# A two-block model on one core: wide feed-forward products, later assumed landings, more idle products at two norms

## Chip, core and metric

One core of a Trainium2 chip runs the whole program, in fp32 data with TensorE's products on operands of type fp32r. The metric is the device time of one execution in microseconds (us). The kernel before was run three times: 1648.75, 1653.19 and 1653.45 us, median 1653.19.

## What is computed

A sequence of 256 tokens of width 1024 goes through a first block (a mixer made of a recurrence and dilated attention, then a feed-forward network) and two second blocks (feed-forward, mixer, feed-forward each). So there are eight sublayers, 0 to 7: mixers are 0, 3 and 6, feed-forward networks 1, 2, 4, 5 and 7. A feed-forward network with its norms and its modulation is, cut to what matters:

```python
h = modulate(rms_norm(x, g_pre), shift, scale)
u, gt = split(h @ w_in, 2)          # 1024 -> 2 x 2816
f = (silu(u) * gt) @ w_out          # 2816 -> 1024
x = x + gate * rms_norm(f, g_post)  # the second block has no rms_norm on f
```

shift, scale and gate come from a product of a condition vector with a matrix (`w_ada`), 24 chunks of 128 values per sublayer.

## The kernel before, in words

Activations lie transposed: a tile is 128 features by 256 tokens. To keep fp32 accuracy every operand is split in two: `hi`, the value rounded by ScalarE to fp32r, and `lo`, what is left, by a subtraction on VectorE (`split`, `load_split`). A product of weights w and activations x is then three matmuls into the same sum, `mm3` (L1022): hi(w)·hi(x), hi(w)·lo(x), lo(w)·hi(x), each with 128x128 weights and 256 moving columns. In the profile's names the weights are `hi` and `lo`; the activations of a network's input are `hh` and `hl` (or `UH` and `UL`, see below), those of its output product `fh` and `fl` (the last eight `fg`), those of a mixer's output `oh` and `ol`.

Weights come in transfers of 512 KB (`raw`, four row chunks by 256 columns), issued in order on SP's queue from one list for the whole program; `fetch` keeps three split ones ahead. Between them stand the transfers of the modulation rows (`ada_step`, from `in_ada`, also 512 KB), each of which VectorE multiplies with the condition and sums (`junk`). None are left for the last feed-forward network.

A feed-forward network (`ffn`, L1253) has NF = 22 units. A unit is a pair of column chunks, one of u and one of gt, over 8 row chunks. The first three units run on `UH`/`UL`, which is x times its scale before the norm's factor is known (`pair_u`, 258 columns); the norm's factor is multiplied in afterwards. The other 19 use `pair` (L1027): the two sums lie side by side in one PSUM bank with the tag `mm`, of which there are two. Behind each unit ScalarE takes silu of the one half (`su`), VectorE multiplies with the other (`fy`), and the result is split (`fh`, `fl`). Then `out_proj` (L1208) makes four pairs of output chunks over 22 row chunks; the last pair uses a bank of `mm` and one of `a`, so that the two end apart.

In the first block (sublayers 0 and 1) the output goes through a norm: a sum over the squares by TensorE into a bank `c`, a logarithm and an exponential on ScalarE (`rstd`), then VectorE multiplies and adds chunk by chunk (`f`, `x`), and ScalarE makes the next `UH`. Meanwhile TensorE runs idle products whose result nobody reads (`keep_warm`, L1123), 14 of 128x256.

The order of the instructions isn't that of the code. All calls on the engines are recorded (`_Engine.record`, L722), with a cost and a time until the result can be used; per sublayer `emit` (L898) tries orders on a model of the engines (`_Stretch.run`) and takes the one with the best score. Each engine then executes its list in order. All recorded instructions therefore have one line in the profile, L725, and are told apart by their tiles.

Of the kernel before, what the change touches and what calls it, by code (L numbers as in the profile page):

```python
# [12 lines left out]
F32 = mybir.dt.float32  # L13
# [12 lines left out]
D = 1024  # L26
# [7 lines left out]
EXPM05 = float(np.exp(np.float64(-0.5)))  # L34

# [582 lines left out]
class _Model:  # L618


    def __init__(self):
        self.at = {"pe": 0.0, "dve": 0.0, "act": 0.0, "pool": 0.0, "dma": 0.0}
        self.uses, self.slots = {}, {}
        self.rec = None
# [54 lines left out]
class _Engine:  # L679
# [42 lines left out]
    def record(self, op, f, a, k):  # L722
# [3 lines left out]
        if op == "dma_start":  # L726
# [3 lines left out]
            if self.name == "dma":  # L730
                return rec.add(_Op("dma", emit, n / 360e3, 0.0), [out], src)
# [56 lines left out]
class _Kernel:  # L788
# [93 lines left out]

    def split(self, y, hi, lo):

        self.act(hi, y)
        self.tt(lo, y, hi.bitcast(F32), SUB)
# [11 lines left out]
    def emit(self, tag, cx):  # L898
# [24 lines left out]
        for stay, lead in rec.starts(tag):  # L923
# [5 lines left out]
            if __import__("os").environ.get("DBG"): print(tag, stay, lead, round(new[0],1), round(best[3],1))  # L929
# [92 lines left out]
    def mm3(self, out, wh, wl, xh, xl, first, last):  # L1022
        self.mm(out, wh, xh, first, False)
        self.mm(out, wh, xl, False, False)
        self.mm(out, wl, xh, False, last)

# [140 lines left out]
    def scaled(self, sub, pool, tag):  # L1167

        self.G = [self.t(pool, [128, S], tag % j) for j in range(KC)]
# [7 lines left out]
    def chunk_hl(self, n, m, j, pool=False):  # L1177
        h = self.t(self.hp, [128, S], "hh%d" % j, F32R)
        l = self.t(self.hp, [128, S], "hl%d" % j, F32R)
        ins = self.act(h, n, AF.Identity, bias=m[:, j:j + 1])  # L1180
        if pool:
            self.nc.gpsimd.tensor_scalar(n, n, 1.0, m[:, j:j + 1], MUL, ADD)
            self.ptt(l, n, h.bitcast(F32), SUB)
        else:
            self.stt(l, n, m[:, j:j + 1], h.bitcast(F32), ADD, SUB)
# [22 lines left out]
    def out_proj(self, nk, H, L, sub, fpool=None):  # L1208
# [21 lines left out]
        for p in range(4):  # L1230
            ps = self.pair(nk, H, L, last=p == 3)
            for c in range(2):
                j = 2 * p + c
                pc = ps[c] if p == 3 else ps[:, c * S:c * S + S]
# [7 lines left out]
        if fpool is not None:  # L1242
            r = self.rstd(self.sums)
            self.behind_r = self.r_ins
            self.keep_warm(14, H[0], self.sums)
# [7 lines left out]
    def ffn(self, sub, n):  # L1253
        tc, nc = self.tc, self.nc
        n_u = 3
        with ExitStack() as rx:
# [4 lines left out]
            def gated(k, y):  # L1261
                h = self.t(fp, [128, S], "fh%d" % k, F32R)
                l = self.t(fp, [128, S], "fl%d" % k if k < NF - KC else "fg%d" % (k - NF + KC), F32R)
                self.split(y, h, l)
# [30 lines left out]
            for k in range(n_u, NF):  # L1295
                if sub == 2 and k == 8:
                    self.rope2_tables(self.pool(rx, "rt2"))
                ps = self.pair(KC, self.H, self.L)
                su = self.t(ft, [128, S], "su")
                self.act(su, ps[:, :S], AF.Silu)  # L1300
                y = self.t(ft, [128, S], "fy")
                self.tt(y, ps[:, S:], su, MUL)
                gated(k, y)
            self.use_table(LNEXP)
            self.out_proj(NF, hh, hl, sub, fp if sub < 2 else None)
            self.emit(sub + 3, rx)

# [84 lines left out]
    def token_loads(self, w, H, L, views, post):  # L1392
# [5 lines left out]
        def quantum(k, q):  # L1398
            def f(hi, lo):
# [3 lines left out]
                for x, (xh, xl) in enumerate(zip(views(H[k]), views(L[k]))):  # L1403
# [13 lines left out]
    def start(self, late):  # L1417
# [15 lines left out]
        for k in range(KC):  # L1433
# [6 lines left out]
            h = self.t(self.hp, [128, S], "hh%d" % k, F32R)  # L1440
# [1027 lines left out]
```

## Time and profile before

| | |
|---|---|
| three runs | 1648.75, 1653.19, 1653.45 us |
| the profiled execution | 1650.98 us |
| its span, first to last instruction | 1648.9 us |
| mean granted clock of TensorE | 0.992 of full |
| TensorE busy | 1581.3 us, 14250 matmuls |
| VectorE busy | 1234.8 us |
| ScalarE busy | 962.2 us |
| moved by DMA | 359.64 MB, mean 218 GB/s |

The profile is of one execution. Busy time of an engine is the union of its instructions; matmuls are pipelined, so that each is shown longer (some 0.28 us) than the distance of their starts. A group of instructions by line shows its count, busy time, mean length and the idle time of the engine ahead of it, with what ended that.

### The profile page before, as it was taken

Reading aid. Unit: us, or ns where it says so; the run is one execution under the profiler, and the core shown is the slowest. Engines: PE = TensorE matmul, PEld = TensorE weight load, DVE = VectorE, ACT = ScalarE, POOL = GpSimd, SP = SyncE. Lnnn points to the kernel's source line nnn. Section 1 sums busy time; section 2 is a strip of 40 time slices with the busy share of each in tenths; the row PEclk is TensorE's granted clock in tenths of the full one; section 3 lists DMA queues with packets and bytes.
Section 4 is the critical chain, followed back from the end, with each engine's and each line's share of the span. In section 5 each row is a group of like instructions: output and inputs, shape, how many; then the busy total and the mean of one; then the engine's idle time right before and its main releaser. Section 6 shows DMA issues by size and latency. Waiting matters only on the chain. (4 is left out here: it accounts for less than half of the span.)

```text
span 1648.9 us, 35735 instructions
## 1 busy us (share of the span) xinstructions
PE 1581.3 (96%) x14250; PEld 1495.3 (91%) x14250; DVE 1234.8 (75%) x2547; ACT 962.2 (58%) x1851; POOL 18.5 (1%) x39
## 2 busy tenths in 40 slices
PE   4999999989999899999999999999999999999998
PEld 4988888889999899999788999999999978899997
DVE  6897775687777797787869877778768887875544
ACT  5674554767444474445697744456454569874542
POOL 0010000000000000000000000000000000000001
PEclk9999999989999999999999999999999999999999
DMA  9645354465888858888524588876888753255552
GB/s 363 254 141 195 101 182 147 134 220 181 292 290 290 285 199 299 281 298 280 173 92 145 184 294 296 277 278 214 300 274 302 278 170 116 82 168 198 182 174 95
DMA packets 102696, 359.64 MB, mean 218 GB/s; under 512 B 11392, under 2 KB 13056, under 8 KB 102528
## 3 DMA queue, kind: packets, MB, share of 16 engines
q1 hardware_dynamic: 102528, 357.34, 63.6%
q8 instruction: 112, 1.84, 0.5%
q14 instruction: 56, 0.46, 0.1%
HBM read 356.25 MB, written 1.05 MB: 217 GB/s over the span
## 5 line engine op out<-in xcount | busy, mean ns | idle before, releaser
L725 DVE TENSOR_TENSOR lo<-raw,hi 128x1024 fp32r<-128x1024 f32 (+2 forms) x478 | 556.3, 1184 | 187.4 <-issue 75.9
L725 ACT ACTIVATE hi<-raw 128x1024 fp32r<-128x1024 f32 (+2 forms) x478 | 486.8, 1026 | 350.7 <-PE ps_mm L725 254.4
L725 PE MATMUL ps_mm<-hh,hi 128*128 128x256 f32 x2040 | 510.0, 286 | 19.2 <-ACT hh L725 9.2
L725 PE MATMUL ps_mm<-hl,hi 128*128 128x256 f32 x2040 | 505.2, 285 | 0.0
L725 PEld LDWEIGHTS ps_mm<-hh,hi 128*128 128x128 f32 x2040 | 387.4, 192 | 27.7 <-DVE fy L725 12.0
L725 PEld LDWEIGHTS ps_mm<-hl,hi 128*128 128x128 f32 x2040 | 387.2, 192 | 2.0 <-issue 0.8
L725 PE MATMUL ps_mm<-hh,lo 128*128 128x256 f32 x2040 | 316.7, 286 | 0.0
L725 DVE CUSTOM_DVE_ANT_0 junk<-raw,cond 128x1024 bf16<-128x1024 f32 x192 | 235.6, 1227 | 64.0 <-DMA raw<-in_ada 63.3
L725 PEld LDWEIGHTS ps_mm<-hh,lo 128*128 128x128 f32 x2040 | 275.7, 193 | 2.9 <-issue 1.1
L725 PE MATMUL ps_mm<-fh,hi 128*128 128x256 f32 x770 | 188.9, 281 | 0.0
L725 PEld LDWEIGHTS ps_mm<-fh,hi 128*128 128x128 f32 x770 | 144.5, 188 | 0.9 <-DVE fy L725 0.9
L725 PE MATMUL ps_mm<-fl,hi 128*128 128x256 f32 x490 | 120.4, 280 | 0.0
L725 PE MATMUL ps_mm<-fh,lo 128*128 128x256 f32 x770 | 115.5, 281 | 2.5 <-DVE lo L725 2.5
L725 PEld LDWEIGHTS ps_mm<-fh,lo 128*128 128x128 f32 x770 | 102.0, 188 | 2.8 <-DVE lo L725 2.8
L725 ACT ACTIVATE fh<-fy 128x256 fp32r<-128x256 f32 x110 | 44.9, 412 | 94.1 <-DVE fy L725 94.1
L725 PEld LDWEIGHTS ps_mm<-fl,hi 128*128 128x128 f32 x490 | 92.2, 188 | 0.0
L725 PE MATMUL ps_mm<-fg,hi 128*128 128x256 f32 x280 | 69.4, 281 | 0.0
L725 PE MATMUL ps_a<-UH,hi 128*128 128x258 f32 x168 | 49.4, 297 | 6.1 <-ACT UH L725 6.1
L725 PEld LDWEIGHTS ps_mm<-fg,hi 128*128 128x128 f32 x280 | 52.7, 188 | 0.0
L725 ACT ACTIVATE su<-ps_mm 128x256 f32<-128x256 f32 x95 | 35.6, 375 | 29.0 <-PE ps_mm L725 28.9
L725 ACT ACTIVATE UH<-x,mod 128x256 fp32r<-128x256 f32 x56 | 26.4, 501 | 43.6 <-DVE x L725 43.6
L725 PE MATMUL ps_a<-UL,hi 128*128 128x258 f32 x168 | 48.9, 293 | 0.0
(559 smaller groups left out, 2631.3 us busy)
## 6 DMA issues: line engine op xcount, KB each, us to landing
raw<-in_ffi SPq DMA_DIRECT2D x220, 512.0 KB, 5.4
raw<-in_ada SPq DMA_DIRECT2D x192, 512.0 KB, 5.3
raw<-in_ffo SPq DMA_DIRECT2D x100, 512.0 KB, 5.1
raw<-in_win SPq DMA_DIRECT2D x66, 512.0 KB, 4.3
raw<-in_wout SPq DMA_DIRECT2D x24, 512.0 KB, 4.1
w<-in_cw SPq DMA_DIRECT2D x16, 512.0 KB, 8.0
raw<-in_ws SPq DMA_DIRECT2D x16, 448.0 KB, 7.5
raw<-in_ffo SPq DMA_DIRECT2D x20, 256.0 KB, 4.0
```

The source lines that it names most:

```text
L725: emit = lambda: f(*a, **k)
```

## The change

It has three parts. In the feed-forward networks' input products behind the first three units, and in the first three output pairs, hi(w)·hi(x) and hi(w)·lo(x) become one matmul of 512 columns: the two halves of an activation now lie in one tile of 128 x 2 x 256 (`parts`), the product writes a whole bank, first half and second half, and lo(w)·hi(x) adds to the first half (`pair_wide`). Each of a pair's two sums then has a bank of its own, both of one tag, and `mm`, `a` and `b` take turns. `halves` adds the two halves of a bank: ScalarE copies the second to SBUF (`wa`), VectorE adds the first. Second, while a feed-forward network is recorded, the ordering model takes a weight transfer to be usable 0.7 us later than its cost says, and one of modulation rows 2 us later. Third, `keep_warm` is called with 34 instead of 14, for both output norms of the first block. The mixers' activations use the new tiles too, but are multiplied as before. The core of the diff:

```diff
 SHIFT = 2560
 HP = HS = 0
 EXPM05 = float(np.exp(np.float64(-0.5)))
+
+
+def low(x):
+
+    return x[:, 1] if len(x.shape) == 3 else x
 
 
 
...
             src = [aps[1]] if aps[1].space == SBUF else []
             n = out.nbytes() if callable(out.nbytes) else out.nbytes
             if self.name == "dma":
-                return rec.add(_Op("dma", emit, n / 360e3, 0.0), [out], src)
+                lag = 0.0
+                if self.model.late_dma and out.shape[-1] == D:
+                    lag = 2.0 if rec.group == 12 else 0.7
+                return rec.add(_Op("dma", emit, n / 360e3, lag), [out], src)
             return rec.add(_Op(self.name, emit, 0.06, 2.2 + n / 360e3), [out], src)
         if not aps:
             return rec.add(_Op(self.name, emit, 1.28, 0.0), [], [])
...
         o, w = self.vat[name]
         return self.vect[:, o + j:o + (w if n is None else j + n)]
 
+    def halves(self, ps, pool):
+
+        t = self.t(pool, [128, S], "wa")
+        self.act(t, ps[:, S:], AF.Copy)
+        self.tt(t, ps[:, :S], t, ADD)
+        return t
+
     def split(self, y, hi, lo):
 
         self.act(hi, y)
...
 
     def mm3(self, out, wh, wl, xh, xl, first, last):
         self.mm(out, wh, xh, first, False)
-        self.mm(out, wh, xl, False, False)
+        self.mm(out, wh, low(xl), False, False)
         self.mm(out, wl, xh, False, last)
+
+    def pair_wide(self, nk, H, L):
+
+
+        tag = self.wide[0]
+        self.wide.rotate(-1)
+        ps = [self.psum(tag) for c in range(2)]
+        for r in range(0, nk, 4):
+            m = min(4, nk - r)
+            hi, lo = self.fetch()
+            for q in range(m):
+                k = r + q
+                for c in range(2):
+                    w = slice(q * 256 + c * 128, q * 256 + c * 128 + 128)
+                    self.mm(ps[c], hi[:, w], L[k].rearrange("p a b -> p (a b)"), k == 0, False)
+                    self.mm(ps[c][:, :S], lo[:, w], H[k], False, k == nk - 1)
+        return ps
+
+    def parts(self, pool, tag, t=None):
+
+        t = self.t(pool, [128, 2, S], tag, F32R) if t is None else t
+        return t[:, 0], t
 
     def pair(self, nk, H, L, tag="mm", last=False):
 
...
 
     def scaled(self, sub, pool, tag):
 
-        self.G = [self.t(pool, [128, S], tag % j) for j in range(KC)]
+        def two(j):
+            g = self.t(pool, [128, 2, S], tag % j)
+            return g[:, 0], g[:, 1]
+
+        self.G = [g for j in range(KC // 2) for g in two(j)]
         for j, g in enumerate(self.G):
             self.act(g, self.x[j], AF.Copy, scale=self.mod(sub)[:, 8 + j:9 + j])
 
...
             rec.late = 0.0
 
         for p in range(4):
-            ps = self.pair(nk, H, L, last=p == 3)
+            two = wide is not None and p < 3
+            ps = self.pair_wide(nk, H, L) if two else self.pair(nk, H, L, last=p == 3)
             for c in range(2):
                 j = 2 * p + c
-                pc = ps[c] if p == 3 else ps[:, c * S:c * S + S]
+                pc = ps[c] if two or p == 3 else ps[:, c * S:c * S + S]
+                if two:
+                    pc = self.halves(pc, wide)
                 if fpool is None:
                     update(j, pc)
                 else:
...
         if fpool is not None:
             r = self.rstd(self.sums)
             self.behind_r = self.r_ins
-            self.keep_warm(14, H[0], self.sums)
+            self.keep_warm(34, H[0], self.sums)
             self.new_sum()
             for j in range(KC):
                 self.tt(f[j], f[j], r, MUL)
...
     def ffn(self, sub, n):
         tc, nc = self.tc, self.nc
         n_u = 3
+        self.model.late_dma = True
+        self.wide = deque(("mm", "a", "b"))
         with ExitStack() as rx:
             fp, ft = (self.pool(rx, "ffn%d%d" % (n, b), b) for b in (1, 2))
             hh, hl = [], []
             pend = []
 
             def gated(k, y):
-                h = self.t(fp, [128, S], "fh%d" % k, F32R)
-                l = self.t(fp, [128, S], "fl%d" % k if k < NF - KC else "fg%d" % (k - NF + KC), F32R)
-                self.split(y, h, l)
+                h, l = self.parts(fp, "fh%d" % k if k < NF - 4 else "fg%d" % (k - NF + 4))
+                self.split(y, h, low(l))
                 hh.append(h)
                 hl.append(l)
 
...
             for k in range(n_u, NF):
                 if sub == 2 and k == 8:
                     self.rope2_tables(self.pool(rx, "rt2"))
-                ps = self.pair(KC, self.H, self.L)
+                ps = [self.halves(p, ft) for p in self.pair_wide(KC, self.H, self.L)]
                 su = self.t(ft, [128, S], "su")
-                self.act(su, ps[:, :S], AF.Silu)
+                self.act(su, ps[0], AF.Silu)
                 y = self.t(ft, [128, S], "fy")
-                self.tt(y, ps[:, S:], su, MUL)
+                self.tt(y, ps[1], su, MUL)
                 gated(k, y)
             self.use_table(LNEXP)
-            self.out_proj(NF, hh, hl, sub, fp if sub < 2 else None)
+            self.out_proj(NF, hh, hl, sub, fp if sub < 2 else None, ft)
             self.emit(sub + 3, rx)
+        self.model.late_dma = False
 
 
     def weave(self, streams, dense=None, share=0.0):
```

What this does to the order is shown at three places. TensorE, in the feed-forward network of sublayer 2, a stretch of the input products; before (`hh` and `hl` are the halves of a chunk, the number tells the chunk's tile):

```order
L725 MATMUL ps_mm<-hh_7750,hi 128x256
L725 MATMUL ps_mm<-hl_7751,hi 128x256
L725 MATMUL ps_mm<-hh_7750,hi 128x256
L725 MATMUL ps_mm<-hl_7751,hi 128x256
L725 MATMUL ps_mm<-hh_7755,hi 128x256
L725 MATMUL ps_mm<-hl_7756,hi 128x256
L725 MATMUL ps_mm<-hh_7755,hi 128x256
L725 MATMUL ps_mm<-hl_7756,hi 128x256
```

and with the change, in the same network:

```order
L732 MATMUL ps_b<-hh_7427,hi 128x512 x2
L732 MATMUL ps_b<-hh_7428,hi 128x512 x2
L732 MATMUL ps_b<-hh_7422,lo 128x256 x2
L732 MATMUL ps_b<-hh_7423,lo 128x256 x2
L732 MATMUL ps_b<-hh_7427,lo 128x256 x2
L732 MATMUL ps_b<-hh_7428,lo 128x256 x2
```

Two matmuls of 256 columns per chunk and sum have become one of 512, now into banks of `b`; the `lo` products stay 256 wide and follow in runs. In all there are 5 x 436 products fewer and 40 idle ones more.

VectorE, in the network of sublayer 4, before:

```order
L725 TENSOR_TENSOR fy<-ps_mm,su 128x256
L725 TENSOR_TENSOR lo<-raw,hi 128x1024
L725 TENSOR_TENSOR fl_12289<-fy,fh_12288 128x256
L725 TENSOR_TENSOR lo<-raw,hi 128x1024
L725 TENSOR_TENSOR fy<-ps_mm,su 128x256
L725 TENSOR_TENSOR lo<-raw,hi 128x1024 x2
L725 TENSOR_TENSOR fl_12302<-fy,fh_12301 128x256
```

and with the change:

```order
L732 TENSOR_TENSOR fy<-wa,su 128x256
L732 TENSOR_TENSOR fh_11676<-fy,fh_11676 128x256
L732 ISA junk,mod_9951<-raw,cond 128x1024
L732 ISA mod_9951 128x1
L732 TENSOR_TENSOR lo<-raw,hi 128x1024 x4
L732 TENSOR_TENSOR wa<-ps_b,wa 128x256 x2
L732 ISA junk,mod_9951<-raw,cond 128x1024
L732 ISA mod_9951 128x1
```

The two additions `wa` of a unit are new; they stand together behind a run of weight splits, and `fy` reads their result and not PSUM.

SP's queue, at the joint of the networks of sublayers 1 and 2 (`in_ffo` are output weights, `in_ffi` input weights, `in_ada` modulation rows), before:

```order
L725 DMA raw<-in_ffo 128x512
L725 DMA raw<-in_ada 128x1024 x2
L725 DMA raw<-in_ffi 128x1024
L725 DMA raw<-in_ada 128x1024
L725 DMA raw<-in_ffi 128x1024
L725 DMA raw<-in_ada 128x1024
L725 DMA raw<-in_ffi 128x1024 x5
```

and with the change:

```order
L732 DMA raw<-in_ffo 128x512
L732 DMA raw<-in_ada 128x1024
L732 DMA raw<-in_ffi 128x1024
L732 DMA raw<-in_ada 128x1024
L732 DMA raw<-in_ffi 128x1024
L732 DMA raw<-in_ada 128x1024 x5
L732 DMA raw<-in_ffi 128x1024 x5
```

Behind the last output weights seven transfers of modulation rows stand ahead of the third input weights, where there were four.

## Rows read from the trace of the kernel before

**Rows 1.** The page: busy time of the engines, and TensorE's clock in 40 slices.

```profile
PE 1581.3 (96%) x14250; PEld 1495.3 (91%) x14250; DVE 1234.8 (75%) x2547; ACT 962.2 (58%) x1851; POOL 18.5 (1%) x39
...
PEclk9999999989999999999999999999999999999999
```

**Rows 2.** Busy time by stretch, input products: stretch, length, engines, clock, DMA share, GB/s.

```profile
597.90:702.70 104.80, 104.14 (x866) 103.29 (x865) 82.00 (x130) 52.73 (x80) 0.00 (x0) 1.00 0.81 279
938.90:1044.10 105.20, 104.30 (x867) 103.25 (x865) 79.82 (x121) 53.21 (x78) 0.00 (x0) 1.00 0.83 283
...
1472.10:1577.00 104.90, 104.21 (x866) 103.25 (x865) 58.76 (x83) 53.26 (x77) 0.00 (x0) 1.00 0.57 188
```

**Rows 3.** The same view, two stretches of output products.

```profile
702.60:765.50 62.90, 62.90 (x530) 62.85 (x530) 49.47 (x73) 28.05 (x38) 0.00 (x0) 1.00 0.81 275
...
1577.00:1639.80 62.80, 62.80 (x529) 62.80 (x530) 30.21 (x37) 24.28 (x31) 4.84 (x7) 1.00 0.43 142
```

**Rows 4.** Timeline of TensorE, 1040 to 1060: start, us, what, count.

```profile
1040.08 3.98 PE L725 MATMUL ps_mm<-hh,lo 128*128 128x256 f32 x32
...
1055.52 3.00 PE L725 MATMUL ps_mm<-fh,lo 128*128 128x256 f32 x24
```

**Rows 5.** Timeline of TensorE, 957 to 960; fourteen steps between second and third.

```profile
957.38 0.38 PE L725 MATMUL ps_mm<-hh,hi 128*128 128x256 f32 x1
957.61 0.28 PE L725 MATMUL ps_mm<-hl,hi 128*128 128x256 f32 x1
...
959.21 0.28 PE L725 MATMUL ps_mm<-hl,hi 128*128 128x256 f32 x1
959.32 1.07 PE L725 MATMUL ps_mm<-hh,lo 128*128 128x256 f32 x8
```

**Rows 6.** Timeline of TensorE, the mixers' 512-column products; twelve steps between second and third.

```profile
820.42 0.86 PE L725 MATMUL ps_mm<-lo,hh 128*128 128x512 f32 x3
1349.04 0.39 PE L725 MATMUL ps_mm<-hi,hh 128*128 128x512 f32 x1
...
1351.80 0.39 PE L725 MATMUL ps_mm<-hi,hh 128*128 128x512 f32 x1
...
1353.37 1.53 PE L725 MATMUL ps_mm<-lo,hh 128*128 128x512 f32 x6
```

**Rows 7.** Timeline of all engines at the second output norm.

```profile
565.96 2.02 PE L725 MATMUL ps_c<-fh 128*128 128x256 f32 x14
...
567.30 2.77 DVE L725 TENSOR_TENSOR f<-f,rstd 128x256 f32<-128x256 f32 x8 [2.09 <-ACT rstd L725]
569.99 2.77 DVE L725 TENSOR_TENSOR x<-f,x 128x256 f32<-128x256 f32 x8
570.45 3.31 ACT L725 ACTIVATE UH<-x,mod 128x256 fp32r<-128x256 f32 x8 [3.18 <-DVE x L725]
571.01 0.58 PE L725 MATMUL ps_a<-UH,hi 128*128 128x258 f32 x1 [3.03 <-ACT UH L725]
```

**Rows 8.** Groups by line, ScalarE, 938.9 to 1044.1: count, busy, mean ns, idle before.

```profile
L725 ACT ACTIVATE hi<-raw 128x1024 fp32r<-128x1024 f32 x38 | 40.3, 1060 | 29.3 <-PE ps_mm L725 26.6 <-DMA raw<-in_ffi 2.7
...
L725 ACT ACTIVATE su<-ps_mm 128x256 f32<-128x256 f32 x18 | 6.8, 375 | 5.6 <-PE ps_mm L725 5.6
```

**Rows 9.** Waits of VectorE from 938.9 to 1044.1.

```profile
DVE junk L725 <- DMA raw<-in_ada: 6.7, 5, 2.0
```

**Rows 10.** Waits of TensorE in the whole span: us, times, longest.

```profile
PE ps_mm L725 <- DVE fy L725: 7.6, 11, 1.9
...
PE ps_mm L725 <- DVE lo L725: 2.5, 1, 2.5
```

**Rows 11.** Busy time by stretch of 4 us at the two output norms.

```profile
364.00:368.00 4.00, 4.00 (x20) 4.00 (x20) 4.00 (x11) 3.85 (x11) 0.00 (x0) 0.50 0.22 87
368.00:372.00 4.00, 4.00 (x26) 3.92 (x25) 2.38 (x7) 2.92 (x5) 0.00 (x0) 0.80 0.02 4
...
572.00:576.00 4.00, 4.00 (x26) 4.00 (x25) 4.00 (x12) 3.29 (x10) 0.00 (x0) 0.70 0.84 339
```

More of the change, by code (lines that the diff above doesn't have):

```diff
@@ L621, in __init__ @@
     def __init__(self):
+        self.late_dma = False
         self.at = {"pe": 0.0, "dve": 0.0, "act": 0.0, "pool": 0.0, "dma": 0.0}
@@ L928, in emit @@
             best = improve(new, best, stay)
-            if __import__("os").environ.get("DBG"): print(tag, stay, lead, round(new[0],1), round(best[3],1))
         last = self.last
@@ L1177, in chunk_hl @@
     def chunk_hl(self, n, m, j, pool=False):
-        h = self.t(self.hp, [128, S], "hh%d" % j, F32R)
-        l = self.t(self.hp, [128, S], "hl%d" % j, F32R)
+        h, l = self.parts(self.hp, "hh%d" % j)
         ins = self.act(h, n, AF.Identity, bias=m[:, j:j + 1])
@@ L1182, in chunk_hl @@
             self.nc.gpsimd.tensor_scalar(n, n, 1.0, m[:, j:j + 1], MUL, ADD)
-            self.ptt(l, n, h.bitcast(F32), SUB)
+            self.ptt(low(l), n, h.bitcast(F32), SUB)
         else:
-            self.stt(l, n, m[:, j:j + 1], h.bitcast(F32), ADD, SUB)
+            self.stt(low(l), n, m[:, j:j + 1], h.bitcast(F32), ADD, SUB)
         self.H.append(h)
@@ L1206, in flush, with out_proj @@
             self.bg.popleft()()
-    def out_proj(self, nk, H, L, sub, fpool=None):
+    def out_proj(self, nk, H, L, sub, fpool=None, wide=None):
         nc = self.nc
@@ L1402, in f @@
                 ws = slice(q * w, q * w + w)
-                for x, (xh, xl) in enumerate(zip(views(H[k]), views(L[k]))):
+                for x, (xh, xl) in enumerate(zip(views(H[k]), views(low(L[k])))):
                     pv = box[x][:, :w]
@@ L1439, in start @@
             self.act(xr[k], xr[k], AF.Identity, scale=gs, bias=shift)
-            h = self.t(self.hp, [128, S], "hh%d" % k, F32R)
-            l = self.t(self.hp, [128, S], "hl%d" % k, F32R)
+            h, l = self.parts(self.hp, "hh%d" % k)
             ins = self.act(h, xr[k])
-            self.tt(l, xr[k], h.bitcast(F32), SUB)
+            self.tt(low(l), xr[k], h.bitcast(F32), SUB)
             self.H.append(h)
@@ L1659, in mixer1 @@
                     self.tt(a1, a1, b1, ADD)
-                    h = self.t(self.hp, [128, S], "hh%d" % j, F32R)
-                    l = self.t(self.hp, [128, S], "hl%d" % j, F32R)
-                    self.split(a1, h, l)
+                    h, l = self.parts(self.hp, "hh%d" % j)
+                    self.split(a1, h, low(l))
                     mH.append(h)
@@ L2322, in finished @@
             def finished(n, po):
-                oH[n] = self.t(p1, [128, S], "oh%d" % n, F32R)
-                oL[n] = self.t(p1, [128, S], "ol%d" % n, F32R)
+                oH[n], oL[n] = self.parts(p1, "oh%d" % n)
                 self.act(oH[n], po[:, :S])
-                self.tt(oL[n], po[:, :S], oH[n].bitcast(F32), SUB)
+                self.tt(low(oL[n]), po[:, :S], oH[n].bitcast(F32), SUB)
             def nsa(j, bank):
```

## The prediction

> **What bounds the kernel now.** The page comes first: TensorE is busy 96% of the span and its clock is at the higher of its two levels (2.4 GHz) in nearly every slice [rows 1]. VectorE's 75% and ScalarE's 58% are averages, so I went on by stage. The change lies in the five feed-forward networks, and each has two long stretches: the input products from the fourth unit on (105 us in three of the rows, [rows 2]) and the output products (62.8 us, [rows 3]). In both, TensorE is busy from end to end, at the full clock, with about 866 and 530 products. So in these stretches the time is the number of products times the spacing of their starts. The other engines must only deliver in time, and what they have to spare is read there too: VectorE is busy 79.8 of 105.2 us in a stretch that still carries the modulation rows, and 58.8 of 104.9 in the last, which doesn't [rows 2].
>
> The third view is the timeline of TensorE, for that spacing. 32 products of 256 columns take 3.98 us: less the last one's 0.28 that is 3.70 / 31 = 119.5 ns from start to start; 24 of the output products give (3.00 - 0.28) / 23 = 118 ns [rows 4]. Just after two longer steps (one is 0.23 us, the others around it 0.12) the same products go faster: 14 steps in 1.60 us, 114 ns, and then eight `lo` products at (1.07 - 0.28) / 7 = 113 ns [rows 5]. I read this as two limits: the array needs 114 ns, and a product with its weight load arrives only every 118 to 120 ns, so that a stock, which could gather during the longer steps, is being used up. Products of 512 columns exist in the mixer's value loads: 12 steps in 2.76 us, 230 ns; runs of six and of three give (1.53 - 0.39) / 5 = 228 and (0.86 - 0.39) / 2 = 235 ns [rows 6].
>
> **The change, part by part.** *Wide products.* A triple of 256-column products (`hi`·h, `hi`·l, `lo`·h) becomes one of 512 and one of 256. Per network there are 19 units x 8 chunks x 2 = 304 such triples in the input products and 3 x 22 x 2 = 132 in the output products; the last output pair and the first three units stay as they are. A triple costs 3 x 119.5 = 359 ns now in the input stretch and 3 x 118.7 = 356 in the output stretch (62.8 us / 529, [rows 3]). For the new one I take 231 + 114 = 345: 231 is the mean of the three values for 512 columns, and 114 is the spacing behind the longer steps, because during a wide product the supply of the next instructions gains as it does there. The saving is 14 ns x 304 = 4.3 us and 11 ns x 132 = 1.5 us, 5.8 us per network, **29 us** for five. Ends: if the wide one takes 235 and the narrow ones stay at 119.5 and 118.7, it is 4 x 304 + 2 x 132 = 1.5 us per network, 7 us in all; with 228 and 113 it is 18 x 304 + 15 x 132 = 7.5 us, 37 us in all.
>
> By the Trainium skill ("TensorE: Matmul & The Clock Gate", section "Back-to-back issue gap") a warm product takes its columns over 2.4 GHz plus a fixed 2.5 ns, and joining two saves that 2.5 ns alone: 436 x 5 x 2.5 ns, an estimate of 5.5 us from that page. The rows here disagree with it at 256 columns (118 to 120 where it gives 109) and at 512 (230 where it gives 216); as a mechanism it returns below as a rival.
>
> *Fetching the two halves.* Each wide pair leaves two sums per bank, so ScalarE copies the second half to SBUF and VectorE adds the first: 44 copies and 44 additions per network, 38 of each in the input stretch. An addition costs VectorE one slot of (2.77 - 0.42) / 7 = 336 ns [rows 7], 12.8 us per input stretch; a copy out of PSUM is 375 ns on ScalarE [rows 8], 14.3 us, which the idle half of that engine covers (53.2 of 105.2 us busy, [rows 2]). VectorE goes from 79.8 of 105.2 to about 92.6 of 100.9 us, and 6.7 us of its idle time in such a stretch is waiting for modulation rows [rows 9]: the cover is nearly used up. TensorE's worst wait for VectorE's split in the kernel is 2.5 us, once [rows 10]. I charge 1 us for each of the four loaded networks, **+4 us**; ends 0 and 2.5 x 4 = 10.
>
> *Three sets of banks.* Before, a unit's sums lie in one of two `mm` banks; now a pair of banks of `mm`, `a` and `b` in turn, so three units are under way. TensorE's waits for `fy` (7.6 us in 11 times, [rows 10]) come from the two banks. The chain behind a unit is longer now by a copy and an addition, so I count half of them as gone, **-3 us**; ends 0 and -7.6.
>
> *34 idle products.* After the second output norm the 14 idle products end near 568, and the first `UH` product starts at 571.01 after 3.03 us of idleness [rows 7], at the lower clock: 0.70 in the mean of 572 to 576; at the first norm it is 0.50 from 364 to 368 and 0.80 to 372 [rows 11]. Twenty more at (2.02 - 0.28) / 13 = 134 ns are 2.7 us: they end near 570.7, before the activation that releases the product, so they cost nothing and leave an idle time of some 0.3 us. If the clock then holds, products that ran slowly no longer do: 20 of them from 364 to 368 and 26 each from 368 to 372 and from 572 to 576 took 4 us each time [rows 11]; at 0.12 us apiece they need 2.4, 3.1 and 3.1, so 1.6 + 0.9 + 0.9 = 3.4 us are to be had at most. VectorE's chain behind the norm (eight steps of 336 ns twice, then `UL`) sets part of that pace, so I take **-2 us**; ends 0 and -3.4.
>
> *Later landings assumed.* This moves transfers on SP's queue and the splits behind them and adds no work. In the input stretches the DMA engines are busy 0.81 to 0.83 of the time at 279 to 283 GB/s [rows 2]; with 5% less time that is 0.87, still short of full. At the stretches' joints more modulation rows stand ahead of the first weight rows than before; the cover is that weights are fetched ahead, and without it this is the third rival. Cost taken: 0. The mixers' own instructions only change places here and there: 0, between -5 and +5.
>
> *Sum.* -29 + 4 - 3 - 2 = -30 us. The profiled execution took 1650.98 us (its span of 1648.9 and 2.1 around it), 2.2 us under the median of 1653.19. **1650.98 - 30 = 1621 us.**
>
> **The rivals.** *Columns set the price.* 512 columns cost what two times 256 cost, in the feed-forward's traffic too: wide ones at 235 and narrow ones still at the supply's pace. For it: 230 is close to twice 114, and one row has 235 [rows 6]. Against it: two rows of three have less, and the spacing of 119.5 is steady over 32 products, which looks like supply and not like the array. Gain 7 us from the products, 3 from the banks and 2 from the clock, less 4: 1643 us. The skill's rule named above ends at about the same place. Chance 0.12.
>
> *VectorE becomes the bound, and it is slower.* The additions stand between the splits in VectorE's queue, two and two, and each first addition waits for a copy that may stand behind a split of 1.06 us on ScalarE [rows 8]; whatever is queued behind it, splits of the next weights and the modulation's sums, waits too. The spare time is 100.9 - 92.6 = 8.3 us in 19 units, 0.44 us per unit. A wait of w us per unit stretches the four loaded input stretches by 19 x (w - 0.44) x 4; from w = 0.83 the 30 us are used up. At w = 1.2, one split and the copy's start, it is 58 us: 1621 + 58 = 1679 us. For it: VectorE at 92%. Against it: the order puts one to four splits ahead of the additions, and VectorE works ahead of TensorE. Chance 0.07.
>
> *The first weight rows of a stretch come late.* At a joint of two stretches SP now issues seven modulation rows, not four, before the third weight row. Three of 524 KB at 283 GB/s are 5.6 us, in four joints 22 us: 1643 us. For it: the order in the queue. Against it: the buffers let the rows be issued early, and the stretch behind a joint is one of little traffic (0.02 to 0.84 of the DMA engines in [rows 11]). Chance 0.09.
>
> **How the numbers follow.** The forecast has the rest, 0.72. Its own range is from -37 - 7.6 - 3.4 (1603 us) to about half of its gain (1637 us); what lies above that is the rivals' ground. To hold 8 in 10 the range must take in the two milder rivals at 1643 and may leave out the slow one: 1603 to 1645. About 0.3% (5 us) is what a measurement of this kernel can tell from no change. Beyond it on the fast side lie nearly all of the forecast (0.70), two thirds of the first rival (0.08) and most of the third (0.07): 0.85. Within 0.3%: 0.07, from the rest of these. Slower: 0.08, the second rival and a joint that goes worse than priced.
>
> **What would show it.** Right: the starts of 512-column products 228 to 235 ns apart in the feed-forward, the 256-column `lo` products behind them 113 to 115 apart and not 119.5; input stretches near 100 us instead of 105 and output stretches near 61.3 instead of 62.8; VectorE busy some 92 us in the loaded input stretches and TensorE without gaps of over a microsecond; granted clock 1.00 behind both output norms. Wrong: `lo` products still at 119.5 (the first rival, and then the supply isn't the limit that I take it for); TensorE waiting on `lo` or on a `wa` addition in every unit (the second); a wait of several us for the first `hi` of a network or of a second-block mixer (the third); idle products that run at half clock or end after the `UH` activation, which would turn the -2 into a loss.

## The result, and the profile after

The changed kernel takes 1624.36 us (median of 4 runs, 1620.56 to 1628.25); the kernel before took 1652.58 beside it. The ratio is 0.9843, with a 95% interval from 0.9819 to 0.9867: 28 us faster by the medians, 22 to 30 by the interval. The profiled execution took 1623.08 us. The forecast was 1621 us. The time came out nearly as forecast; its parts did not, and the experiments show that two wrong terms nearly cancelled, so that the total is in part luck.

The page of the changed kernel answers to [rows 1]: busy time of the engines, and TensorE's clock in 40 slices.

```profile
PE 1560.8 (96%) x12110; PEld 1386.9 (86%) x12110; DVE 1307.9 (81%) x2767; ACT 1030.6 (64%) x2071; POOL 17.9 (1%) x39
...
PEclk9999999999999999999999999999999999999999
```

Busy time by stretch answers to [rows 2, 3]: three whole input stretches, then two of output products (stretch, length, PE, PEld, DVE, ACT, POOL, clock, DMA share, GB/s).

```profile
579.00:685.20 106.20, 106.20 (x611) 93.45 (x610) 96.69 (x176) 68.55 (x122) 0.00 (x0) 1.00 0.77 262
917.40:1023.70 106.30, 106.30 (x611) 93.47 (x610) 90.34 (x155) 65.15 (x114) 0.00 (x0) 1.00 0.80 268
1442.20:1549.90 107.70, 107.70 (x623) 94.92 (x622) 75.67 (x129) 66.89 (x117) 0.00 (x0) 1.00 0.57 187
685.20:747.20 62.00, 62.00 (x398) 56.20 (x397) 54.42 (x85) 30.95 (x48) 0.43 (x3) 1.00 0.82 282
1549.90:1611.80 61.90, 61.90 (x397) 56.06 (x396) 32.93 (x48) 26.47 (x40) 4.29 (x7) 1.00 0.43 144
```

The first two rows hold 304 pairs of products each (608, and three neighbours): 106.2 us / 304 = 349 ns for what three products did before. From first to last product the same two stretches took 113.4 and 113.8 us before the change, with 24 products on `UH` and `UL` in between; [rows 2] begin a little later and hold some 866 of the 912 products. VectorE is busy 91% of the first one, the loaded end of what the prediction feared, and TensorE still has no gap there.

TensorE's timeline shows the pace (start, us, what, count), as [rows 4 to 6] did.

```profile
640.33 2.08 PE L732 MATMUL ps_a<-hh,lo 128*128 128x256 f32 x16
...
645.08 1.07 PE L732 MATMUL ps_b<-hh,lo 128*128 128x256 f32 x8
...
650.10 2.22 PE L732 MATMUL ps_a<-hh,hi 128*128 128x512 f32 x9
```

The wide ones start (2.22 - 0.39) / 8 = 229 ns apart; the narrow ones (2.08 - 0.28) / 15 = 120 in a long run and 113 in the short run of eight. Over the whole stretch of 579.0 to 685.2 the starts lie 230 ns and 119 ns apart (287 steps of each): **230 + 119 = 349**. The prediction had 231 + 114.

TensorE's longest waits behind its cold start, from 360 to 1640 us, answer to [rows 10] (us, times, longest): `fy` and the feed-forward's `lo` are gone.

```profile
PE ps_a L732 <- DMA w<-in_cw: 4.9, 2, 4.3
PE ps_b L732 <- ACT P0b L732: 2.7, 3, 1.3
PE ps_c L732 <- DVE acc L732: 2.6, 2, 2.2
PE ps_a L732 <- ACT hi L732: 2.5, 1, 2.5
```

At the second output norm, for [rows 7], the idle products now end just ahead of `UH`; the wait is 0.63 us where it was 3.03, and behind it the clock is 1.00 where [rows 11] had 0.70:

```profile
552.74 1.96 PE L732 MATMUL ps_c<-fh 128*128 128x256 f32 x15
...
555.33 0.39 PE L732 MATMUL ps_a<-UH,hi 128*128 128x258 f32 x1 [0.63 <-ACT UH L732]
```

```profile
553.40:557.40 4.00, 3.37 (x28) 3.17 (x28) 4.00 (x13) 2.63 (x7) 0.00 (x0) 1.00 0.95 329
557.40:561.40 4.00, 3.97 (x33) 3.77 (x32) 4.00 (x10) 2.63 (x8) 0.00 (x0) 1.00 1.01 388
561.40:565.40 4.00, 1.80 (x6) 1.50 (x7) 2.93 (x11) 2.23 (x4) 0.00 (x0) 0.86 1.00 381
```

The last of these windows is a new hole: TensorE waits 2.23 us for the sum of squares, because VectorE's additions to `acc` stand between modulation sums (`junk`):

```profile
561.98 1.22 DVE L732 CUSTOM_DVE_ANT_0 junk<-raw,cond 128x1024 bf16<-128x1024 f32 x1
563.12 0.09 DVE L732 DVE_READ_ACCUMULATOR2_ANT mod<- 128x1 f32 x1
563.12 0.42 DVE L732 TENSOR_TENSOR acc<-acc,sq 128x256 f32<-128x256 f32 x1
```

Where the time went, from the profiled execution of each kernel. "Input" is the sum over the five networks from the fifth product on `UH` or `UL` to the first output product, "output" from there to the last output product, "rest" is what is left of the span: mixers, norms, the start, and the first four products of each network (some 2.6 us in all with 34 idle products, 3.0 to 3.5 with 14). The ratio is the measure across sets, since each set had its own runs of the kernel before.

| kernel | input | output | rest | span | median, ratio to before |
|---|---|---|---|---|---|
| before | 654.6 | 315.7 | 678.6 | 1648.9 | 1652.58 |
| the change | 627.4 | 309.0 | 684.9 | 1621.3 | 1624.36, 0.9843 |
| 14 idle products | 627.4 | 309.0 | 686.1 | 1622.5 | 1626.30, 0.9858 |
| no later landings | 633.1 | 320.2 | 685.6 | 1638.9 | 1639.99, 0.9935 |
| wide products alone | 640.5 | 312.8 | 679.4 | 1632.7 | 1636.27, 0.9923 |
| later landings alone | 645.3 | 312.2 | 681.2 | 1638.7 | 1640.81, 0.9948 |
| landings of modulation rows only | 630.7 | 309.4 | 675.6 | 1615.7 | 1618.20, 0.9803 |
| two pairs of banks | 628.8 | 309.5 | 683.9 | 1622.2 | 1622.79, 0.9837 |
| no copy and addition | 625.1 | 309.5 | 679.8 | 1614.4 | 1620.49, 0.9823 |
| narrow products of 128 columns | 640.8 | 305.3 | 714.9 | 1661.0 | 1658.23, 1.0046 |
| the change, repeated | 627.3 | 309.3 | 694.2 | 1630.8 | 1623.76, 0.9846 |

The networks gave 33.9 us and the rest took 6.3 back. The two rows of the same changed kernel differ by 9.3 us in the rest and by 0.4 in the networks: one execution says nothing about a mixer below some 9 us, and much about a network.

### The profile page after: what moved, and what is told of

It reads as the page before. It is cut to its first block, busy times and chain, and to the rows that moved or that the text cites. A ratio compares the mean times of both kernels' runs of the same rounds, so it can differ in the third digit from the quotient of the medians.

```text
span 1621.3 us, 32120 instructions
## 1 busy us (share of the span) xinstructions
PE 1560.8 (96%) x12110; PEld 1386.9 (86%) x12110; DVE 1307.9 (81%) x2767; ACT 1030.6 (64%) x2071; POOL 17.9 (1%) x39
## 4 chain that ended last, share of the span: by engine, by line
PE 68%; ACT 5%; DVE 5%; issue 1%; DMA 1%; DVEq 0%; SPq 0%; ACTq 0%
PE ps_mm L732 25%; PE ps_a L732 23%; PE ps_b L732 19%; PE ps_c L732 1%; ACT P1b L732 1%; ACT P1a L732 1%; DVE lo L732 1%; ACT P0b L732 1%; ACT P0a L732 1%; DVE UL L732 0%; DMA w<-in_cw 0%; ACT hi L732 0%; DVE x L732 0%; DVE f L732 0%; DVE junk L732 0%
## 5 line engine op out<-in xcount | busy, mean ns | idle before, releaser
L732 PE MATMUL ps_mm<-hh,hi 128*128 128x256 f32 (+1 forms) x1600 | 310.8, 328 | 9.9 <-ACT hh L732 7.9
L732 PEld LDWEIGHTS ps_mm<-hh,hi 128*128 128x128 f32 x1600 | 247.7, 192 | 37.4 <-ACT hh L732 8.8
L732 PE MATMUL ps_mm<-hh,lo 128*128 128x256 f32 x1080 | 173.0, 286 | 0.0
L732 PEld LDWEIGHTS ps_mm<-hh,lo 128*128 128x128 f32 x1080 | 149.6, 192 | 4.0 <-issue 0.5
L732 PE MATMUL ps_a<-hh,hi 128*128 128x512 f32 (+1 forms) x560 | 137.5, 378 | 0.0
L732 PE MATMUL ps_b<-hh,hi 128*128 128x512 f32 (+1 forms) x544 | 131.3, 380 | 0.0
L732 PEld LDWEIGHTS ps_a<-hh,hi 128*128 128x128 f32 x560 | 101.2, 191 | 18.5
L732 PEld LDWEIGHTS ps_b<-hh,hi 128*128 128x128 f32 x544 | 96.7, 189 | 17.5
L732 PE MATMUL ps_mm<-fh,hi 128*128 128x512 f32 (+1 forms) x360 | 82.6, 337 | 0.0
L732 PEld LDWEIGHTS ps_mm<-fh,hi 128*128 128x128 f32 x360 | 60.3, 188 | 6.4
```

Of the source, the lines that this page charges most:

```text
L732: emit = lambda: f(*a, **k)
```

## The experiments

**The three parts by themselves.** Three kernels undo one part or two, a fourth adds the landings to the kernel before.

```diff
-            self.keep_warm(34, H[0], self.sums)
+            self.keep_warm(14, H[0], self.sums)
```

> The change with 14 idle products instead of 34 at the two norms, the rest as in the change. Theory (the prediction's -2 us): the twenty are free and keep the clock. Then TensorE stands idle for about 3 us before the first UH product again (0.9 us in the changed kernel), its clock is lower in the 4 us behind that, and the time is 2 to 3.4 us longer, about 1626.5 us. Rival (they buy nothing): the products behind the norms wait for VectorE's chain anyway, the time is the changed kernel's 1624.4 within 1 us. Second rival (they run into the UH product): the time is 1 us or more shorter.

```diff
-        self.model.late_dma = True
+        self.model.late_dma = False
```

> The change with the assumption of later landings switched off. Theory A (the new order of the transfers gives back at the joints): the input stretches keep their 106 us, and the stretches between the feed-forward networks, longer by 3.3, 3.2 and 4.7 us in the changed kernel, go back to what they were; the time is 5 to 11 us shorter, 1613 to 1619 us. Theory B (the later landings pay): VectorE waits for modulation rows as before the change (63 us over the span where it is 14 now), TensorE waits on lo, hi or fy again, the input stretches are 1 to 3 us longer each, and the time is 3 to 10 us longer, 1627 to 1634 us. Theory C (the prediction's 0): within 2 us of 1624.4; the joints' loss then comes from the wide products and the copies.

The third makes both edits:

> The kernel before with the 512-column products alone: 14 idle products, no later landings. By the trace of the changed kernel a triple takes 349 ns where it took 359, 10 ns x 304 + 8 x 132 a network, 20 us in five networks, and TensorE's waits for fy (7.6 us) are gone: about 1625 us if the other two parts are worth nothing, 1627 if the idle products are worth their 2 us. If theory A on the landings holds it is 5 to 11 us faster than that, if theory B holds 3 to 10 us slower. The prediction's own number for this part is -29 + 4 - 3, that is 1623 us.

The fourth is the kernel before with the `lag` lines and the two settings of `late_dma` from the diff:

> The kernel before with the later landings alone: 256-column products throughout, 14 idle products. Theory (the later landings pay only where VectorE is nearly full, that is together with the wide products' additions and shorter stretches): in the kernel before TensorE waits for lo 2.5 us and for fy 7.6 us, the latter for its two pairs of banks; so 0 to 4 us are to be had, the joints take some of it, and the time is 1647 to 1652 us against some 1650 us before. Rival (the later landings are worth their 12 us in any kernel): 1636 to 1641 us, with input stretches some 2 us shorter each.

Measured: 0.9858 [0.9840, 0.9876] with 14 idle products, 0.9935 [0.9921, 0.9949] without later landings, 0.9923 [0.9905, 0.9941] with the wide products alone, 0.9948 [0.9934, 0.9961] with the landings alone. So the wide products with their copies and banks are worth 14 us by the medians (1650.14 to 1636.27), not the forecast 29 - 4 + 3 = 28; the later landings, forecast at 0, are worth 10 alone (1651.12 to 1640.81) and 10 more on the wide products (1636.27 to 1626.30). Theory B on the landings holds, with more than its 3 to 10 us; and on the kernel before the rival holds (1636 to 1641 us), against my theory that the landings pay only in company. In the networks alone the landings give 12.8 us without wide products and 16.9 with them. No kernel without the landings was run with another seed of the planner; but the two with wide products and no landings have the same sum over the networks, 953.3 us, and the nine with both (narrow products of 256 columns) lie between 934.6 and 942.0.

The trace shows how. This is VectorE's timeline in the kernel with wide products alone:

```profile
469.78 0.09 DVE L732 DVE_READ_ACCUMULATOR2_ANT mod<- 128x1 f32 x1
474.60 1.23 DVE L732 CUSTOM_DVE_ANT_0 junk<-raw,cond 128x1024 bf16<-128x1024 f32 x1 [4.73 <-DMA raw<-in_ada]
475.75 0.08 DVE L732 DVE_READ_ACCUMULATOR2_ANT mod<- 128x1 f32 x1
475.75 1.22 DVE L732 TENSOR_TENSOR lo<-raw,hi 128x1024 fp32r<-128x1024 f32 x1
476.89 0.75 DVE L732 TENSOR_TENSOR wa<-ps_b,wa 128x256 f32<-128x256 f32 x2
```

and TensorE's at the same place:

```profile
472.66 2.00 PE L732 MATMUL ps_a<-hh,hi 128*128 128x512 f32 x8
477.02 2.06 PE L732 MATMUL ps_a<-hh,lo 128*128 128x256 f32 x8 [2.36 <-DVE lo L732]
```

VectorE stands 4.73 us in front of a modulation row that hasn't landed; the split behind it in the queue is ready to go, and TensorE waits 2.36 us for it. The kernel before does the same with `fy`:

```profile
409.12 1.22 DVE L725 CUSTOM_DVE_ANT_0 junk<-raw,cond 128x1024 bf16<-128x1024 f32 x1 [4.49 <-DMA raw<-in_ada]
410.27 0.08 DVE L725 DVE_READ_ACCUMULATOR2_ANT mod<- 128x1 f32 x1
410.27 1.22 DVE L725 TENSOR_TENSOR lo<-raw,hi 128x1024 fp32r<-128x1024 f32 x1
411.41 0.42 DVE L725 TENSOR_TENSOR fy<-ps_mm,su 128x256 f32<-128x256 f32 x1
```

```profile
411.88 0.39 PE L725 MATMUL ps_mm<-hh,hi 128*128 128x256 f32 x1 [1.85 <-DVE fy L725]
```

VectorE's waits of this kind over the span (us, times, longest). In the kernel before:

```profile
DVE junk L725 <- DMA raw<-in_ada: 63.3, 40, 4.5
```

With the landings alone:

```profile
DVE junk L726 <- DMA raw<-in_ada: 28.0, 19, 3.5
```

With the wide products alone:

```profile
DVE junk L732 <- DMA raw<-in_ada: 73.0, 32, 4.8
```

And in the change:

```profile
DVE junk L732 <- DMA raw<-in_ada: 14.2, 11, 3.4
```

With the landings alone TensorE's waits for `fy` and `lo` fall from 7.6 + 2.5 to 2.2 + 0; that is 8 of the 12.8 us, the rest I couldn't put down to single waits. Not all of them stand behind a modulation row. In the kernel before, VectorE's last idle time ahead of the wait was in front of a modulation row for the 2.5 us on `lo` and for five of the eleven waits on `fy`, 3.7 of 7.6 us. Four more, 3.3 us, lie near the heads of the input stretches, where VectorE had last stood idle for ScalarE's `su`; one of them is in the last network, which has no modulation rows:

```profile
1475.97 0.48 DVE L725 SCALAR_TENSOR_TENSOR fy<-ut,usc,su 128x256 f32<-128x256 f32 x1 [1.01 <-ACT su L725]
1480.31 0.50 PE L725 MATMUL ps_mm<-hh,hi 128*128 128x256 f32 x2 [0.69 <-DVE fy L725]
```

The 2.2 us that the landings alone leave are two waits at such heads.

The twenty idle products came out at -2.5 us (0.9858 to 0.9843) with the landings and at +2 (0.9923 to 0.9935) without: nothing that these runs can tell from zero, though with 34 the holes at the norms (3.0 us each again with 14) are gone as forecast.

**Which landing.** The lag of modulation rows alone:

```diff
-                    lag = 2.0 if rec.group == 12 else 0.7
+                    lag = 2.0 if rec.group == 12 else 0.0
```

> The change with the later landing assumed for the modulation rows alone (2.0 us), not for the weight rows (0). By the runs so far the two together are worth some 12 to 15 us. Theory (the cost is VectorE standing still in front of a modulation row, with splits and wa additions queued behind it): the rows alone bring nearly all of it. VectorE's waits for modulation rows stay under 20 us over the span (they are 73 to 87 us without any later landing), TensorE has no waits for lo or wa in the feed-forward, and the time is 1622 to 1628 us. Rival (a split that waits for its weight row holds up the queue just as much): waits for lo come back and the time is 1630 to 1638 us.

0.9803 [0.9788, 0.9818], 1618.20 us, below the theory's range. The modulation rows bring it all: VectorE's waits for them are 7.2 us, and TensorE waits for neither `lo` nor `wa`. It is even faster than the change, but its networks are 3.7 us longer, nearly all in the second one, where TensorE waits 3.26 us for a `hi` at 565.00; what it gains lies in the rest. The last set returns to that.

**The third pair of banks.**

```diff
-        self.wide = deque(("mm", "a", "b"))
+        self.wide = deque(("mm", "a"))
```

> The change with two pairs of banks in turn in place of three. The prediction's -3 us for the third pair: TensorE waits for fy or for a wa addition some microseconds in a stretch again (7.6 us in all before), and the time is 3 us longer, 1627 us, at most 7.6. Rival (the chain behind a unit is now longer by a copy and an addition, so two pairs are far too few): TensorE waits in nearly every unit, 0.5 us or more in each of 95, and the time is 20 us or more longer. Second rival (two are enough): no such waits, 1624.4 within 1 us.

0.9837 [0.9817, 0.9856]: the second rival. Two pairs are enough, although the chain behind a unit is longer than before; the networks lose 1.9 us, the median nothing (1622.79 is 1.6 under the change, which these runs can't tell from the theory's 1). TensorE waits for `fy` and `wa` not once. So two units under way don't bring the `fy` waits of [rows 10] by themselves; about half of them came from VectorE standing at modulation rows. The waits at the heads are gone in all kernels with wide products; which part of that change removes them isn't shown.

**The copies and additions.** The sum of the first half is used alone:

```diff
-        t = self.t(pool, [128, S], "wa")
-        self.act(t, ps[:, S:], AF.Copy)
-        self.tt(t, ps[:, :S], t, ADD)
-        return t
+        return ps[:, :S]
```

> The change without the copy and the addition of the second half: the sum of the first 256 columns is used as it is, so the products of the second half stay but are left out of the result. This prices the prediction's +4 us. Theory (TensorE never waits for wa in the changed kernel, so they are hidden): 1624.4 us within 2 us; VectorE is busy some 220 x 0.34 = 74 us less over the span. Rival (they still cost at the ends of the stretches, or the order pays for them): 4 to 10 us shorter, 1614 to 1620 us.

0.9823 [0.9805, 0.9841], 1620.49 us. The median, 3.9 us shorter (3.3 by the ratios, whose intervals overlap), lies between the two theories, so the stages decide. VectorE is busy 72 us less (1235.9 against 1307.9). The input products behind the first three units take 531.9 us in all networks against 531.7, the output products 309.5 against 309.0; the 1.8 us that the networks gain come from the three units behind the second norm (20.5 us against 23.1). In the stretches, where the +4 was charged, the copies and additions are hidden.

**What sets the narrow product's 119 ns.**

```diff
-                    self.mm(ps[c][:, :S], lo[:, w], H[k], False, k == nk - 1)
+                    self.mm(ps[c][:, :128], lo[:, w], H[k][:, :128], False, k == nk - 1)
```

> The change with the narrow products at 128 columns in place of 256: the second half of the tokens is left out of the products with lo in the wide pairs (2180 of them). It asks what sets the narrow product's 119 ns. Theory of the prediction (each product with its load of weights is supplied only every 118 to 120 ns): they stay 115 to 120 ns apart and the time stays within 5 us of 1624.4. Rival (the columns set the price): they go to 57 to 66 ns, the input stretches fall from 106 to 88 to 92 us, where VectorE's 92 us of work in a loaded stretch bounds them, and the time is 1535 to 1570 us. A third reading, a floor in between from the load of weights, would show as a spacing of 70 to 110 ns.

1.0046 [1.0027, 1.0065]: half the columns, and slower than before. Two things came out. First the price, in TensorE's timeline of this kernel:

```profile
656.41 2.07 PE L732 MATMUL ps_b<-hh,hi 128*128 128x512 f32 x8
658.32 1.00 PE L732 MATMUL ps_b<-hh,lo 128*128 128x128 f32 x8
659.16 2.04 PE L732 MATMUL ps_mm<-hh,hi 128*128 128x512 f32 x8
```

Sorted by place in a run (590 to 685 and 950 to 1040 us), the starts of 128-column products lie 111.7 ns apart from the second step on, through the ninth and later; only the first step of a run is short, 58 ns, and the first of the next wide run is as much longer, 284 instead of 230. So the spacing has a floor of 112 ns that columns don't set, and it is there at once: no stock of loaded weights gathers during wide products to be used up later. The trace of the kernel before already had it, in the mixers' products of 32 columns, whose starts are 112 ns apart from the second step on:

```profile
1345.39 0.98 PE L725 MATMUL ps_a<-kcb,q 128*128 128x32 f32 x8
```

In the changed kernel the same sorting gives 115 ns for the first narrow step and 118 to 119 from the second to the last. The 111.7 ns lie between the first reading's 115 to 120 and the third's 70 to 110, in neither; the rival's 57 to 66 is out, and so is the prediction's 114 behind wide products. Every product of these kernels has its own load of weights (14250 of each, [rows 1]), so no run tells the load from another cost per product. By the Trainium skill ("TensorE: Matmul & The Clock Gate", section "LDWEIGHTS (loading the stationary operand)") a load of weights takes its columns over 1.2 GHz, an estimate of 106.7 ns for 128 columns from that page; the 111.7 agrees with it within 5%. The same page's sustained 81 ns for 128 columns (section "Back-to-back issue gap") does not hold for these products; it gives that figure for pairs of load and product, and calls the formula that the prediction took from it one for a product by itself. The input stretches became 2.0 us shorter in the mean (531.7 to 521.5 us in five), as 304 x 7 ns say.

Second, why it was slower: TensorE waits 44.6 us in 4 places, each time for the first `hi` behind a run of modulation rows at a joint. SyncE's queue and ScalarE at the second norm:

```profile
546.55 26.80 SPq L732 DMA_DIRECT2D raw<-in_ada  x8
573.40 2.86 SPq L732 DMA_DIRECT2D raw<-in_ffi  x5
```
```profile
579.18 1.06 ACT L732 ACTIVATE hi<-raw 128x1024 fp32r<-128x1024 f32 x1 [6.99 <-DMA raw<-in_ffi]
```

These eight modulation rows (and one at 544.47) stand ahead of the next weight rows, and their issue takes 26.8 us, since SyncE waits there for VectorE: from 544 to 574 us 10.8 us for modulation sums and 13.0 for `acc`, and 5.6 for landings. That is the prediction's third rival, in full and at twice its price. The edit changed the durations that the planner sees and so its order; at the joints of the changed kernel no more than five modulation rows stand in one run.

**How much is luck of the order.** The change again; the change with another seed of the planner's scoring; modulation rows only with that seed; and modulation rows only, in the mixers too.

> The changed kernel once more, word for word, beside the three others of this set: 1624 us, between 1620 and 1628, is what both theories of the set give; it is the measure for them.

```diff
-        rng = np.random.RandomState(0)
+        rng = np.random.RandomState(1)
```

> The changed kernel with another seed for the random lengthening of steps by which the planner scores its candidate orders; no instruction is added, removed or resized. It asks how far re-planning alone moves the time, because the mixers and joints differed by up to 10 us in all between kernels whose edits do not touch them. Theory (re-planning is worth some microseconds): the input and output stretches keep 106 and 62 us, the mixers' and joints' sum moves by 2 to 10 us either way, and the time lies between 1615 and 1634 us but not within 1 us of the changed kernel's. Rival (the orders are much the same): within 1 us.

> The later landing for the modulation rows alone, which gave 1618 us against 1624 us, with the other seed. Theory (those 6 us were won in the mixers by the luck of the order; the weight rows' own 0.7 us are worth nothing): the time is that of the seed run of the changed kernel within 5 us, and lies between 1615 and 1632 us. Rival (leaving the weight rows at 0 really is better): 4 us or more faster than the changed kernel with this seed, about 1618 us again.

```diff
-        self.late_dma = False
+        self.late_dma = True
...
-                    lag = 2.0 if rec.group == 12 else 0.7
+                    lag = 2.0 if rec.group == 12 else 0.0
...
-        self.model.late_dma = False
```

> A candidate for a better version: the later landing for the modulation rows alone, and in the mixers' orders too, not only in the feed-forward's. Theory (VectorE stands before modulation rows in the mixers also; a true landing time there saves some of it): 2 to 8 us faster than 1618, that is 1610 to 1616 us. Rival (the mixers are bound by chains of other waits, for P0b, for hi and for the cw rows, and few modulation rows run there): 1618 us within the 5 us of re-planning, 1613 to 1624 us.

Measured: 0.9846 [0.9818, 0.9875]; 0.9869 [0.9841, 0.9896]; 0.9839 [0.9807, 0.9870]; 0.9875 [0.9849, 0.9902]. The other seed moves the median by 4.5 us (1623.76 to 1628.30), as the theory has it, though the two intervals overlap, and the networks by 0.2: what re-planning does, it does in mixers and norms. The modulation rows alone were 6 us faster than the change with the one seed and 5.6 with the other, past both the theory's 5 and the rival's 4, but with intervals that touch or overlap, and in stretches that the edit doesn't touch. It is the fastest version measured, 1618.2 us; that leaving the weight rows' lag at 0 makes it so isn't shown. Carrying the landings into the mixers lost that again (1630.71 us); my theory for it fell, the rival's 1613 to 1624 too, and the cause stays open.

## Why the prediction was right, and where it was wrong

**The sum.** -30 us forecast; -28 measured, by the medians (1652.58 to 1624.36). Its terms:

| term | forecast | measured |
|---|---|---|
| wide products | -29 | about -20, from the spacings |
| fetching the halves | +4 | 0 in the stretches, under 4 at a norm |
| three pairs of banks | -3 | -2 to +2 |
| idle products | -2 | between -2.5 and +2 |
| later landings | 0 | -10 by the medians; -13 to -17 in the networks |
| mixers | 0, ±5 | +6 in the profiled run, -3 to +16 in the others with networks like the change's |

By the medians the first three rows together, forecast at -28, gave -14 to -15 (1650.14 to 1636.27, and 0.9948 to 0.9858 with the landings), in the networks -17 to -21. They were some 13 us short of the forecast by the medians and the landings 10 us beyond it, so that the total came so near is luck.

*Wide products.* 231 ns for 512 columns was right (230). The step that failed is "114 is the spacing behind the longer steps, because during a wide product the supply of the next instructions gains as it does there". Narrow products stay at 119. That leaves 359 - 349 = 10 ns a triple: 304 x 10 and 132 x 7 ns, five times, 20 us; between the kernel with landings alone and the one with 14 idle products the networks differ by 21.1. The first rival had the narrow price right and the wide one wrong (235), so the truth lay between it and the forecast. [Rows 5] did show 113 to 114; I took a short run for a rule, and the eight products at 113 in the changed kernel's timeline show that such runs still occur. What makes them is open. (3.70 / 31 is 119.4 and not 119.5; that is under 1 us of the 29.)

*Later landings.* The step that failed is "moves transfers on SP's queue and the splits behind them and adds no work ... Cost taken: 0". It moved more than transfers: VectorE's modulation sums now stand later in its order, behind work that was ready. [Rows 9] showed 6.7 us of waiting in one stretch, and I entered them as spare time of VectorE. They were the cause of some 6 of TensorE's 10 us of waits for `fy` and `lo`, since VectorE takes its instructions in order.

*Banks.* "TensorE's waits for `fy` come from the two banks" was the same mistake from the other end: the name of the last releaser, `fy`, was read as the cause, and the wait ahead of it on VectorE wasn't looked up. [Rows 10] had the time and the times; the row at 409.12 shows the reason for about half of them.

*Halves.* Nothing in the stretches, because the landings free VectorE. Without them (wide products alone) TensorE waits for `lo` 5.5 us and for `wa` 2.7: the second rival in its mild form. "The cover is nearly used up" was right, and the other part of the change restored it.

*Idle products.* The mechanism came out as forecast at the first norm: they end ahead of `UH`, and the granted clock is 1.00 in the 8 us behind it, where the kernel with 14 has 0.50 and 0.68. From the first `UH` product to the first output product the first network takes 126.2 us for 128.3. At the second norm the kernel with 14 has the clock at 1.00 too, in spite of a hole of 3.03 us, where the kernel before had 0.70 (one execution each), and with 34 that network takes 129.7 us for 127.4, with a wait for `acc` of 2.23 us where the other has 0.6. The forecast 2 us can't be seen in the medians.

*Third rival.* In the changed kernel it shows once, mildly. Ahead of the last mixer five modulation rows take SyncE 14.16 us, TensorE waits 2.47 us for the `hi` behind them, and its granted clock is 0.60 in the 4 us after that:

```profile
1260.75 14.16 SPq L732 DMA_DIRECT2D raw<-in_ada  x5
1281.35 0.58 PE L732 MATMUL ps_a<-UH,hi 128*128 128x258 f32 x1 [2.47 <-ACT hi L732]
1281.30:1285.30 4.00, 3.95 (x21) 3.95 (x22) 3.94 (x5) 3.11 (x4) 0.00 (x0) 0.60 1.00 399
```

From the last output product to the next network that mixer takes 153.2 us for 147.7 before, and 153.7 in the repeat, which has the same wait: a part of the 6 us that the mixers lost. The kernel with 128-column products shows the mechanism in full.

## What to carry to other kernels

Where an engine takes its work in order and one of its inputs comes by DMA, follow a wait to the instruction in front of the late one: a modulation row that the planner believed landed held up splits that were ready, and correcting that one assumed time was worth 10 us of 1650, as much as two thirds of the wide products. Price a merged product from rows of both widths over whole stretches and not from a short run. And where a planner orders the work, change its seed once before believing any difference of a few microseconds outside the edited stretches.

## What was not expected of the hardware

A product with its own load of weights takes 112 ns at 32 columns and at 128, and 119 at 256, so halving 256 columns saves 7 ns; 512 columns take 230. A narrow product here is nearly all a price that its columns don't set, and merging two that share weights saves 8 of 238 ns. The products stay between 113 and 120 ns (256 columns) and 226 and 236 ns (512) by something that no run here settles.
